# A hybrid encoder step on one core: attention in the source's order, value differences beside the gated mixer, keys first

## The chip, the cores and the metric

The kernel runs on one NeuronCore of one Trainium2 chip. The metric is the time of one execution on the device, in microseconds (us). Below, PE is TensorE, DVE is VectorE, ACT is ScalarE, POOL is GpSimd, and SP is the queue that issues most transfers.

## The reference

One layer of a streaming encoder works on 1024 prompt rows and 32 sample rows of width 1024:

```
xn     = RMSNorm(h);  u_a, u_b, v_b, q, k, v, gates = split(xn @ w_in)
y_a    = S5(u_a)                 # diagonal complex state space, scan over time, GELU, GLU
y_b    = u_b * (tril(W_s) @ LayerNorm(v_b) + b_s)          # gated mixer, chunks of 128
y_c    = stick_breaking(q, k, v)                           # 8 heads x 64, strictly causal
merged = sum_i sigmoid(gates_i) * (y_i @ w_branch_i);  h += merged @ w_out
h     += (silu(g) * u) @ w_down,  g, u = split(RMSNorm(h) @ w_gate_up);  y = RMSNorm(h)
```

Stick-breaking weights a value with sigmoid(z) times the product of (1 - sigmoid(z)) over the later keys. The outputs include keys, values and S5's final states.

## The kernel before, in words

Dense products are made three times in fp32r, with high and low parts of both operands (`mm3`, L143 to L146); weights are loaded, rounded on ACT (L117) and their rest is taken on POOL (L118) in a ring of four.

Phase 1 (L204 to L1060) projects the values (`v_dense`), then runs three things in the source's order: the S5 set-up on DVE (`s5_setup`), the gated mixer (`sgu`, nine blocks), the S5 main stage (`ua_dense`, `s5_main`), and then `attention`. Beside them runs filler: `tasks` holds four key/query tasks (`qk_dense`, one per pair of heads) and eleven gate tasks (`gate_ahead`). `fill(us)` (L1021) takes steps from the first task until their nominal cost, 3n/2400 us for n columns, has used up the credit; `finish` runs a task to its end. Before the change, the first two key/query tasks are finished before the mixer, the others are filler beside the mixer and S5. Tile's scheduler then orders each engine's instructions by source position and by its own forecast of readiness, so an instruction can come ahead of others that wait. SBUF pools that are closed give their place to later ones, and a tile waits for the tiles whose place it takes.

`qk_dense` splits keys and queries into high and low parts (`qe`, L325 to L330) and stores them by SP (L332). `s5_setup` builds S5's direct matrix D by sixteen transfers from `KK` (L632). `s5_main` loads U in eight transfers (L654), multiplies (L661), scans on DVE (L671 to L697), makes y (L708 to L710), stores and reloads it (L721, L726), and rounds it (`yh`, L729).

`attention` (L762) works in 32 units (pair of heads, pair of 128-row blocks tp, head). `stage_a` makes the scores of two row blocks on PE (L823 to L827), the sigmoid of minus the score on ACT (L829), and the reversed running product on DVE (L831, `om`). `stage_b` makes, for each pair of key blocks, a `turn` (four transposes, L853; their high part on ACT, L861; their low part on DVE, L862) and one turn later an `apply` (four products with the value differences, L870 and L871). It works with differences of neighbouring values: per head `load_values` loads two shifted copies (L780, L781) and `differences` makes them (L786 to L790). The next unit's `stage_a` steps are put between the turns of this one. `sample_attention` (L952) comes before the last unit; `while tasks: fill(1.0)` then runs what filler is left.

Phase 2 (L1065 on) loads the branch outputs y (L1095) and weighs them with the gates; three units of gate 7 come first there.

Of the kernel before, what the change touches and what calls it, by code (L numbers as in the profile page):

```python
# [9 lines left out]
F32 = mybir.dt.float32  # L10
F32R = mybir.dt.float32r
# [37 lines left out]
def trunk_kernel(ctx: ExitStack, tc: tile.TileContext,  # L49
# [32 lines left out]
    v_d = [dram.tile([TP + 1, 128], F32, name=f"v_d{i}") for i in range(4)]  # L82
    vs_d = dram.tile([32, 512], F32, name="vs_d")
# [120 lines left out]
    with ExitStack() as ph1:  # L204
# [3 lines left out]
        kk = ph1.enter_context(pool("kk", 1))  # L208
# [82 lines left out]
        def qk_dense(wk, hp):  # L291
# [22 lines left out]
            for which in (1, 0):  # L314
                unit = next_unit(768 + 512 * which + 128 * hp)
                dst = (q_d, k_d)[which][hp]
                for h, o, n, t0 in CHUNKS:
# [7 lines left out]
                    qe = wk.tile([128, 2, 512], F32R, name="qe", bufs=2)  # L325
# [30 lines left out]
        def sgu(wk, WT, BB, gs):  # L356
            pt = ps_tile("t")
            for i in range(4):
# [3 lines left out]
                            compare_op=OP.is_ge, fill=0.0)  # L362
            VN = wk.tile([128, 9, 256], F32, name="VN")
            us = tm_units(win, 512)
            for b, (t0, rows, h, off) in enumerate(BLOCKS):
# [20 lines left out]
                fill(1.5)  # L386
            for ft in range(2):
# [33 lines left out]
        def s5_setup(pl, keep, out):  # L421
# [185 lines left out]
            KK = pl.tile([32, 8, 128], F32, name="KK", tag="big")  # L607
# [154 lines left out]
        def attention(at, qk_tasks):  # L762
            cnt = [0]

            last = at.tile([128, 1], F32, name="last")
            v.tensor_scalar(last, ident[:, 127:128], -1.0, None, op0=OP.add)
# [6 lines left out]
            def load_values(hp, h2):  # L773

                va = at.tile([128, 12, 64], F32, name="va", bufs=1)
                vt = at.tile([128, 12, 2, 64], F32R, name="vt", bufs=3)
                vb = vt[:, :, 1, :].bitcast(F32)
                for tl, r0 in ((va, 0), (vb, 1)):
                    src = v_d[hp][r0:r0 + TP, 64 * h2:64 * h2 + 64].rearrange("(b s) c -> s b c", s=128)
                    sp.dma_start(tl[:, 0:8], src)  # L780
                    sp.dma_start(tl[:, 8:12], src[:, 1::2])  # L781
                return va, vt

            def differences(va, vt):
                vb = vt[:, :, 1, :].bitcast(F32)
                v.tensor_sub(va[:, 0:8], va[:, 0:8], vb[:, 0:8])  # L786

                v.scalar_tensor_tensor(va[:, 8:12], vb[:, 8:12], last, va[:, 8:12], op0=OP.mult, op1=OP.add)
                s.activation(vt[:, :, 0, :], va, AF.Copy)
                v.tensor_sub(vt[:, :, 1, :], va, vt[:, :, 0, :].bitcast(F32))  # L790
# [3 lines left out]
            diags = [[at.tile([128, 512], F32R, name=f"wd{i}{e}") for e in range(2)] for i in range(2)]  # L794
# [5 lines left out]
            raw_values = []  # L800
# [8 lines left out]
            def stage_a(hp, tp, h2):  # L809
                kst = heads[hp, h2][0]  # L810
                q2 = qs.pop((hp, tp, h2))
                ws = []
                for tt in range(2):
                    i = 2 * tp + tt
                    n = 128 * (i + 1)
                    cs = ((0, max(n, 256)),) if n <= 512 else (((0, 384), (384, 256)) if n == 640 else
                                                             ((0, 384), (384, 384)) if n == 768 else
                                                             ((0, 512), (512, n - 512)))
                    om = at.tile([128, 1024], F32, name="om", bufs=4)
                    for c0, w in cs:  # L820
                        z = ps_tile("z")
                        last = c0 + w >= n
                        pe.matmul(z[:, 0:w], q2[:, 0, 128 * tt:128 * tt + 128], kst[:, c0:c0 + w], start=True, stop=False)  # L823
                        pe.matmul(z[:, 0:w], q2[:, 1, 128 * tt:128 * tt + 128], kst[:, c0:c0 + w], start=False, stop=not last)
                        if last:
                            d0 = n - 128 - c0
                            pe.matmul(z[:, d0:d0 + 128], identb, maskb, start=False, stop=True)  # L827
                        e = min(w, n - c0)
                        s.activation(om[:, c0:c0 + e], z[:, 0:e], AF.Sigmoid, scale=-0.125)  # L829
                    rev = om[:, 0:n][:, ::-1]  # L830
                    v.tensor_tensor_scan(rev, rev, rev, 1.0, op0=OP.mult, op1=OP.bypass)  # L831
                    ws.append(om)
                    yield ws, 2 * n / 2400.0 + 0.06

            avs = {}

            def stage_b(hp, tp, h2, ws):
                vt = heads[hp, h2][1]
                if h2 == 0:
# [3 lines left out]
                hl = {}  # L843

                def turn(p):

                    pt = ps_tile("t")
                    diag = p == tp
                    for e in range(4):
                        if diag and e == 0:  # L850
                            continue
                        sb, tt = 2 * p + 1 - e // 2, e % 2
                        pe.transpose(pt[:, 128 * e:128 * e + 128], ws[tt][:, 128 * sb:128 * sb + 128], ident)  # L853
                    lo = 128 if diag else 0
                    if diag:
                        wh, wl = diags[cnt[0] % 2]
                        cnt[0] += 1
                    else:
                        wh = at.tile([128, 512], F32R, name="wth", bufs=2)
                        wl = at.tile([128, 512], F32R, name="wtl", bufs=2)  # L860
                    s.activation(wh[:, lo:512], pt[:, lo:512], AF.Copy)  # L861
                    v.tensor_sub(wl[:, lo:512], pt[:, lo:512], wh[:, lo:512].bitcast(F32))  # L862
                    hl[p] = wh, wl

                def apply(p):
                    wh, wl = hl.pop(p)
                    for i in range(2):
                        b = 8 + p if p == tp and i == 0 else 2 * p + 1 - i
                        lhs = vt[:, b].rearrange("p l d -> p (l d)")
                        pe.matmul(av, lhs, wh[:, 256 * i:256 * i + 256], start=(p == 0 and i == 0), stop=False)  # L870
                        pe.matmul(av, lhs, wl[:, 256 * i:256 * i + 256], start=False, stop=(p == tp and i == 1))  # L871

                for p in range(tp + 1):
                    turn(p)
                    yield 0.44
                    if p:
                        apply(p - 1)
                        yield 0.44
                apply(tp)
                if h2:  # L880
# [5 lines left out]
                    v.tensor_sub(yo[:, 1], ty, yo[:, 0].bitcast(F32))  # L886
                    o = 256 * (tp % 2)
                    for e in range(2):
                        sp.dma_start(y_d[4 + hp][tp // 2].rearrange("l p t -> p l t")[64 * e:64 * e + 64, :, o:o + 256],
                                     yo[:, :, 256 * e:256 * e + 256].bitcast(F32))  # L890
                yield 0.44

            units = [(hp, 3 - tp if hp == 3 else tp, h2) for hp in range(4) for tp in range(4) for h2 in range(2)]
            ratio = 0.7

            def run_a(u):
                for ws, c in stage_a(*u):
                    fill(ratio * c)
                return ws

            def ahead(i):

                if i < len(units):
                    hp, tp, h2 = units[i]
                    new = (hp, h2) not in heads
                    if new:
                        finish(qk_tasks[hp])
                        heads[hp, h2] = [load_head(hp, h2)]
                    load_q(hp, tp, h2)
                    if new:  # L910
                        while raw_values:
                            differences(*raw_values.pop())
                        pair = load_values(hp, h2)
                        heads[hp, h2].append(pair[1])
                        raw_values.append(pair)
                        return
                while raw_values:
                    differences(*raw_values.pop())
# [4 lines left out]
            ws = run_a(units[0])  # L923
            for i, u in enumerate(units):
                ahead(i + 2)
                nxt, done = None, True
                if i + 1 < len(units):
                    nxt = stage_a(*units[i + 1])
                    done = False
                for c in stage_b(*u, ws):  # L930
                    fill(ratio * c)
                    if not done:
                        try:
                            wn, c = next(nxt)
# [368 lines left out]
```

## Time and profile before

| | |
|---|---|
| median of 3 runs | 1789.54 us (1789.34 to 1792.63) |
| profiled execution | 1793.48 us, span 1791.7 us |
| PE, DVE, ACT, POOL busy | 95%, 39%, 29%, 30% of the span |
| mean granted PE clock | 0.974 of 2.4 GHz |
| PE waits before attention (75 to 450 us), listed | 28.7 us |
| PE waits from 450 to 705 us, listed | 26.2 us |

Times in rows are us from the span's start. "x8" counts instructions, and an arrow reads out<-in. A busy PE need not be at its peak: matmuls overlap, and their ends are modelled.

### The profile page before, as it was taken

The page shows a single profiled execution, that of the slowest core. Times are in us where ns is not written, and L with a number is a line of the kernel's source. Part 1 is how long each engine was busy: PE and PEld are TensorE (multiplying, and loading weights), DVE is VectorE, ACT ScalarE, POOL GpSimd, SP SyncE. Part 2 cuts the span into 40 slices and gives each one's busy share as a digit, 9 for nine tenths or more (in the row PEclk, how much of TensorE's full clock was granted, in tenths as well). Part 3 has the DMA queues.
Part 4 walks back from the last instruction along what each step waited for, and adds up shares of the span by engine and source line. Part 5 has one row for each costly group of instructions (what it writes and reads, how often), then busy time and mean ns, then how long its engine had stood idle before and what let it go on. Part 6 is the DMA issues. An engine that isn't in the chain of part 4 may idle for free.

```text
span 1791.7 us, 25639 instructions
## 1 busy us (share of the span) xinstructions
PE 1697.7 (95%) x10421; PEld 1504.1 (84%) x10421; DVE 698.9 (39%) x1396; ACT 520.7 (29%) x914; POOL 541.1 (30%) x333
## 2 busy tenths in 40 slices
PE   6988998999889899999999899999999999999997
PEld 6977897778677788899999798888889889888885
DVE  7962523312699840820275602131131230221215
ACT  4322332123466632222333321112112112111124
POOL 2210221334010323434452233333233323333344
PEclk9988999699999999999999999999999999999999
DMA  7453245255666526753362211111111111111112
GB/s 221 115 131 76 85 129 126 69 155 174 172 145 162 150 78 217 255 192 97 92 205 60 59 48 48 48 48 48 48 46 49 36 36 48 48 48 48 48 32 90
DMA packets 246575, 178.18 MB, mean 99 GB/s; under 512 B 60148, under 2 KB 223000, under 8 KB 246456
## 3 DMA queue, kind: packets, MB, share of 16 engines
q1 hardware_dynamic: 217896, 161.32, 31.1%
q10 hardware_dynamic: 28560, 15.21, 2.9%
q8 instruction: 82, 1.34, 0.3%
q14 instruction: 37, 0.30, 0.1%
HBM read 136.69 MB, written 39.21 MB: 98 GB/s over the span
## 4 chain that ended last, share of the span: by engine, by line
PE 75%; DVE 14%; issue 4%; DMA 3%; ACT 2%; POOL 1%; SPq 1%; POOLq 0%; ACTq 0%; DVEq 0%
PE p L146 18%; PE p L145 18%; PE p L144 18%; DVE om L831 4%; PE p_d L144 3%; PE p_d L146 3%; PE p_d L145 3%; PE p_av L144 2%; PE p_av L146 2%; PE p_av L145 2%; DVE rs_m L169 1%; DVE wtl L862 1%; PE p L1245 1%; DMA raw<-in_w_in_dram 1%; POOL wl L118 1%
## 5 line engine op out<-in xcount | busy, mean ns | idle before, releaser
L118 POOL TENSOR_TENSOR wl<-raw,wh 128x1024 fp32r<-128x1024 f32 x164 | 409.0, 2501 | 887.4 <-ACT wh L117 847.1
L145 PE MATMUL p<-x,wh 128*128 128x272 f32 (+1 forms) x1056 | 342.2, 324 | 0.0
L146 PE MATMUL p<-x,wl 128*128 128x272 f32 (+1 forms) x1056 | 341.4, 323 | 0.0
L144 PE MATMUL p<-x,wh 128*128 128x272 f32 (+1 forms) x1056 | 341.2, 323 | 0.0
L117 ACT ACTIVATE wh<-raw 128x1024 fp32r<-128x1024 f32 x164 | 172.6, 1060 | 463.8 <-PE p L146 178.9
L1201 DVE TENSOR_TENSOR sl<-p,sl 128x272 f32<-128x272 f32 (+1 forms) x66 | 34.7, 525 | 463.8 <-PE p L146 463.8
L144 PEld LDWEIGHTS p<-x,wh 128*128 128x128 f32 x1056 | 198.7, 188 | 16.0
L145 PEld LDWEIGHTS p<-x,wh 128*128 128x128 f32 x1056 | 198.7, 188 | 15.9
L146 PEld LDWEIGHTS p<-x,wl 128*128 128x128 f32 x1056 | 198.5, 188 | 15.2
L144 PE MATMUL p_d<-xnh,wh 128*128 128x272 f32 (+1 forms) x464 | 158.5, 342 | 10.9 <-ACT vb L377 7.2
L146 PE MATMUL p_d<-xnh,wl 128*128 128x272 f32 (+1 forms) x464 | 155.8, 336 | 4.7 <-POOL wl L118 4.7
L145 PE MATMUL p_d<-xnl,wh 128*128 128x272 f32 (+1 forms) x464 | 155.4, 335 | 0.0
L1204 POOL TENSOR_TENSOR act<-sl,act 128x512 fp32r<-128x512 f32 (+2 forms) x66 | 61.0, 925 | 278.7 <-ACT act L1202 278.7
L1255 DVE TENSOR_TENSOR h<-p,h 128x512 f32<-128x512 f32 x160 | 108.2, 687 | 79.2 <-PE p L146 79.2
L145 PE MATMUL p<-wl,act 128*128 128x512 f32 x352 | 137.2, 390 | 1.2 <-POOL wl L118 1.2
L146 PE MATMUL p<-wh,act 128*128 128x512 f32 x352 | 137.1, 389 | 0.0
L144 PE MATMUL p<-wh,act 128*128 128x512 f32 x352 | 136.9, 389 | 0.0
L144 PEld LDWEIGHTS p_d<-xnh,wh 128*128 128x128 f32 x464 | 90.1, 194 | 20.0 <-ACT vb L377 7.4
L146 PEld LDWEIGHTS p_d<-xnh,wl 128*128 128x128 f32 x464 | 89.6, 193 | 13.3 <-POOL wl L118 6.0
L145 PEld LDWEIGHTS p_d<-xnl,wh 128*128 128x128 f32 x464 | 90.2, 194 | 7.3
L831 DVE TENSOR_TENSOR_SCAN om<-om 128x128 f32<-128x128 f32 (+3 forms) x64 | 88.8, 1399 | 17.5 <-ACT om L829 17.4
L1202 ACT ACTIVATE act<-sl 128x272 fp32r<-128x272 f32 (+1 forms) x66 | 32.6, 494 | 189.7 <-DVE sl L1201 189.7
(414 smaller groups left out, 3360.3 us busy)
## 6 DMA issues: line engine op xcount, KB each, us to landing
raw<-in_w_in_dram SPq DMA_DIRECT2D x66, 512.0 KB, 3.9
raw<-in_w_gate_up_dram SPq DMA_DIRECT2D x44, 512.0 KB, 3.8
raw<-in_w_down_dram SPq DMA_DIRECT2D x22, 512.0 KB, 3.5
q<-q_d SPq DMA_DIRECT2D x64, 128.0 KB, 2.9
raw<-in_w_out_dram SPq DMA_DIRECT2D x16, 512.0 KB, 6.1
sig_d<-sga ACTq DMA_DIRECT2D x21, 256.0 KB, 2.7
sgg<-sig_d SPq DMA_DIRECT2D x21, 256.0 KB, 3.5
y<-y_d SPq DMA_DIRECT2D x16, 272.0 KB, 4.7
```

The source lines that it names most:

```text
L117: s.activation(wh, raw, AF.Copy)
L118: g.tensor_sub(wl, raw, wh.bitcast(F32))
L144: pe.matmul(ps, ah, bh, start=start, stop=False)
L145: pe.matmul(ps, ah, bl, start=False, stop=False)
L146: pe.matmul(ps, al, bh, start=False, stop=stop)
L169: v.scalar_tensor_tensor(t, y, mh, y, op0=OP.mult, op1=OP.mult)
L831: v.tensor_tensor_scan(rev, rev, rev, 1.0, op0=OP.mult, op1=OP.bypass)
L862: v.tensor_sub(wl[:, lo:512], pt[:, lo:512], wh[:, lo:512].bitcast(F32))
L1201: v.tensor_mul(sl[:, 0:n], pu, sl[:, 0:n])
L1202: s.activation(act[:, e, t0:t0 + n], sl[:, 0:n], AF.Copy)
L1204: g.tensor_sub(act[:, e, T + TS + t0:T + TS + t0 + p], sl[:, 0:p], act[:, e, t0:t0 + p].bitcast(F32))
L1255: v.tensor_add(hr[:, cs], ps, hr[:, cs])
```

## The change

Attention's instructions on PE and DVE are kept in the source's order (a manual schedule for those two engines). `stage_a` becomes `scores(u, tt)`; a unit's turns are followed by the next unit's two score blocks, and products come two turns after their transposes, across units, so there are three buffers for the high and low parts and three diagonal pairs. `fill` takes 2.0 nominal us per unit. The output's last subtraction and its stores come one turn later. Sample attention comes behind the last unit.

The value differences are made beside the gated mixer, one head per block, in a pool `vd` with one buffer of each kind, written to DRAM (`dv_d`) in one transfer per head and loaded in one in attention. All four key/query tasks are finished before the mixer, and the pool of their keys is closed there. The gates' prefetch is three units deep in the S5 main stage, where it was two, and the split keys have three buffers, where they had two.

```diff
+    dv_d = [dram.tile([128, 12, 2, 64], F32, name=f"dv_d{i}") for i in range(NH)]
...
-                    qe = wk.tile([128, 2, 512], F32R, name="qe", bufs=2)
+                    qe = wk.tile([128, 2, 512], F32R, name="qe", bufs=3)
...
+            def load_values(i):
+                va = vk.tile([128, 12, 64], F32, name="vda")
+                vt = vk.tile([128, 12, 2, 64], F32R, name="vdt")
+                for r0, tl in enumerate((va, vt[:, :, 0, :].bitcast(F32))):
+                    src = v_d[i // 2][r0:r0 + TP, 64 * (i % 2):64 * (i % 2) + 64].rearrange("(b s) c -> s b c", s=128)
+                    sp.dma_start(tl[:, 0:8], src)
+                    sp.dma_start(tl[:, 8:12], src[:, 1::2])
+                held.append((i, va, vt))
+            def differences():
...
+                v.tensor_sub(va[:, 0:8], va[:, 0:8], vb[:, 0:8])
+                v.scalar_tensor_tensor(va[:, 8:12], vb[:, 8:12], last, va[:, 8:12], op0=OP.mult, op1=OP.add)
+                s.activation(hi, va, AF.Copy)
+                v.tensor_sub(vt[:, :, 1, :], va, hi.bitcast(F32))
+                sp.dma_start(dv_d[i], vt.bitcast(F32))
...
                 fill(1.5)
+                if held:
+                    differences()
+                if b < 8:
+                    load_values(b)
...
-            KK = pl.tile([32, 8, 128], F32, name="KK", tag="big")
+            KK = pl.tile([32, 8, 128], F32, name="KK", tag="tg")
...
             def load_values(hp, h2):
...
+                sp.dma_start(vt.bitcast(F32), dv_d[2 * hp + h2])
+                return vt
...
             for i, u in enumerate(units):
                 ahead(i + 2)
+                nxt = units[i + 1] if i + 1 < len(units) else None
+                wn = []
+                part = beside / (u[1] + 2)
+                for p in range(u[1] + 1):
+                    held.append(turn(u, ws, p))
+                    if nxt and len(wn) < 2:
+                        wn.append(scores(nxt, len(wn)))
+                    if late:
+                        store()
+                    if len(held) > 2:
+                        apply(*held.pop(0))
+                    fill(part)
+                if nxt and len(wn) < 2:
+                    wn.append(scores(nxt, len(wn)))
+                fill(part)
+                qs.pop(u)
+                ws = wn
+            for h in held:
+                fill(2)
...
+                apply(*h)
...
+            sample_attention(at)
...
+                finish(qk_tasks[3])
+            with pool("sgu", 1) as sg, pool("vd", 1) as vk:
+                sgu(sg, vk, *sgc)
             with pool("s5m", 1) as s5m:
                 ua_dense(s5m)
-                unit_depth[0] = 2
+                unit_depth[0] = 3
                 s5_main(s5m, S)
         early[0] = False
+        with pool("at", 1) as at, tc.manual_schedule(engines={mybir.EngineType.PE, mybir.EngineType.DVE}):
+            attention(at)
```

## Rows read from the trace of the kernel before

**Rows 1.** Timelines of ACT and PE: start, duration, instruction, at the segments' ends

```profile
139.78 0.38 ACT L326 ACTIVATE qe<-p_d 128x272 fp32r<-128x272 f32 x1
...
249.16 0.27 ACT L648 ACTIVATE ua<-p_av 128x32 f32<-128x32 f32 x1
...
291.08 0.68 PE L661 MATMUL p_z<-U,BT 128*64 128x133 f32 x8
...
450.38 0.36 PE L823 MATMUL p_z<-kst,q 128*128 128x256 f32 x1 [1.80 <-DMA q<-q_d]
...
700.18 0.72 PE L144 MATMUL p<-xnh,wh 128*128 128x512 f32 x1 [2.00 <-ACT wh L117]
```

**Rows 2.** Waits of PE, 75 to 450 us: total, times, longest

```profile
PE p_d L144 <- ACT vb L377: 7.2, 1, 7.2
PE p_t L305 <- ACT kt L307: 7.0, 1, 7.0
```

**Rows 3.** Windows: length, busy PE, PEld, DVE, ACT, POOL, then PE clock, DMA share, GB/s

```profile
169.20:180.00 10.80, 10.79 (x69) 10.79 (x70) 9.45 (x57) 4.92 (x20) 0.00 (x0) 0.75 0.01 2
180.00:249.40 69.40, 68.15 (x481) 61.70 (x480) 29.66 (x78) 22.07 (x47) 14.76 (x7) 1.00 0.30 94
...
460.00:480.00 20.00, 18.73 (x109) 14.78 (x110) 14.50 (x19) 10.70 (x22) 0.00 (x0) 1.00 0.68 176
500.00:520.00 20.00, 16.58 (x102) 14.93 (x103) 16.63 (x22) 9.19 (x19) 5.04 (x2) 0.83 0.51 124
```

**Rows 4.** Waits of PE, 450 to 705 us

```profile
PE p_av L871 <- DVE wtl L862: 13.7, 17, 2.8
PE p_t L853 <- DVE om L831: 6.1, 14, 0.9
```

**Rows 5.** Timeline of ACT: ends of filler chunks (idle before in brackets), and yh

```profile
399.45 0.60 ACT L1014 ACTIVATE sga<-p_d 128x512 f32<-128x512 f32 x1 [4.98 <-PE p_d L146]
...
402.42 1.98 ACT L729 ACTIVATE yh<-U 128x2144 fp32r<-128x2144 f32 x1
...
686.14 0.40 ACT L1014 ACTIVATE sga<-p_d 128x272 f32<-128x272 f32 x1 [2.61 <-PE p_d L146]
```

**Rows 6.** Timeline of SP: first and last of U's loads, and y's reload

```profile
255.12 0.42 SPq L654 DMA_DIRECT2D U<-us_d  x1
...
282.20 2.81 SPq L654 DMA_DIRECT2D U<-us_d  x3
...
386.07 0.45 SPq L726 DMA_DIRECT2D U<-ys_d  x1
```

**Rows 7.** DMA issues: count, KB each, median us from issue to landing

```profile
kst<-k_d SPq DMA_DIRECT2D x8, 512.0 KB, 4.5
...
va<-v_d SPq DMA_DIRECT2D x8, 256.0 KB, 7.7
vt<-v_d SPq DMA_DIRECT2D x8, 256.0 KB, 5.3
...
U<-us_d SPq DMA_DIRECT2D x8, 134.0 KB, 4.9
```

**Rows 8.** Tile va in 450 to 672 us (busy DVE, ACT); a scan's group by line

```profile
450.00:672.00 222.00, 18.63 (x24) 6.73 (x8) 0.98 0.54 140
...
L831 DVE TENSOR_TENSOR_SCAN om<-om 128x1024 f32<-128x1024 f32 x8 | 19.6, 2445 | 0.0
```

**Rows 9.** Tile p_d (filler's PSUM) from the first score to 672 us: PE, PEld, DVE, ACT

```profile
450.40:672.00 221.60, 82.40 (x436) 64.65 (x437) 0.00 (x0) 7.74 (x18) 0.98 0.54 140
```

**Rows 10.** Groups of POOL and DVE by line, 640 to 672 us

```profile
L980 POOL TENSOR_SCALAR_AFFINE_SELECT sgs<-sgs 32x32 f32<-32x32 f32 x8 | 1.7, 208 | 1.8 <-ACT sgs L974 1.5
...
L983 DVE TENSOR_TENSOR_SCAN oms<-oms 128x160 f32<-128x160 f32 x2 | 1.0, 492 | 13.6 <-POOL oms L980 13.6
```

**Rows 11.** Timeline of SP at the end of attention

```profile
679.62 12.93 SPq L1095 DMA_DIRECT2D y<-y_d  x16
692.84 1.60 SPq L113 DMA_DIRECT2D raw<-in_w_in_dram  x2
```

More of the change, by code (lines that the diff above doesn't have):

```diff
@@ L807, in load_q, with scores @@
                 qs[hp, tp, h2] = q2
-            def stage_a(hp, tp, h2):
+            def scores(u, tt):
+                hp, tp, h2 = u
                 kst = heads[hp, h2][0]
[L811 to L833, printed above, removed]
@@ new lines, in scores @@
+                for c0, w in cs:
+                    z = ps_tile("z")
+                    last = c0 + w >= n
+                    pe.matmul(z[:, 0:w], q2[:, 0, 128 * tt:128 * tt + 128], kst[:, c0:c0 + w], start=True, stop=False)
+                    pe.matmul(z[:, 0:w], q2[:, 1, 128 * tt:128 * tt + 128], kst[:, c0:c0 + w], start=False, stop=not last)
+                    if last:
+                        d0 = n - 128 - c0
+                        pe.matmul(z[:, d0:d0 + 128], identb, maskb, start=False, stop=True)
+                    e = min(w, n - c0)
+                    s.activation(om[:, c0:c0 + e], z[:, 0:e], AF.Sigmoid, scale=-0.125)
@@ new lines, in scores, with store @@
+                rev = om[:, 0:n][:, ::-1]
+                v.tensor_tensor_scan(rev, rev, rev, 1.0, op0=OP.mult, op1=OP.bypass)
+                return om
+            avs = {}
+            late = []
+            def store():
+                (hp, tp, h2), yo, ty = late.pop()
+                v.tensor_sub(yo[:, 1], ty, yo[:, 0].bitcast(F32))
+                o = 256 * (tp % 2)
+                for e in range(2):
+                    sp.dma_start(y_d[4 + hp][tp // 2].rearrange("l p t -> p l t")[64 * e:64 * e + 64, :, o:o + 256],
+                                 yo[:, :, 256 * e:256 * e + 256].bitcast(F32))
@@ new lines, in turn @@
+            def turn(u, ws, p):
+                tp = u[1]
+                pt = ps_tile("t")
+                diag = p == tp
+                for e in range(4):
+                    if diag and e == 0:
+                        continue
+                    sb, tt = 2 * p + 1 - e // 2, e % 2
+                    pe.transpose(pt[:, 128 * e:128 * e + 128], ws[tt][:, 128 * sb:128 * sb + 128], ident)
+                lo = 128 if diag else 0
+                if diag:
+                    wh, wl = diags[cnt[0] % 3]
+                    cnt[0] += 1
+                else:
+                    wh = at.tile([128, 512], F32R, name="wth", bufs=3)
+                    wl = at.tile([128, 512], F32R, name="wtl", bufs=3)
+                s.activation(wh[:, lo:512], pt[:, lo:512], AF.Copy)
+                v.tensor_sub(wl[:, lo:512], pt[:, lo:512], wh[:, lo:512].bitcast(F32))
+                return u, p, wh, wl
@@ L840, in stage_b, with apply @@
+            def apply(u, p, wh, wl):
+                hp, tp, h2 = u
+                if (hp, tp) not in avs:
                     avs[hp, tp] = ps_tile("av")
@@ L842, in stage_b @@
                 av = av2[:, 256 * h2:256 * h2 + 256]
[L843 to L880, printed above, removed]
+                vt = heads[hp, h2][1]
+                for i in range(2):
+                    b = 8 + p if p == tp and i == 0 else 2 * p + 1 - i
+                    lhs = vt[:, b].rearrange("p l d -> p (l d)")
+                    pe.matmul(av, lhs, wh[:, 256 * i:256 * i + 256], start=(p == 0 and i == 0), stop=False)
+                    pe.matmul(av, lhs, wl[:, 256 * i:256 * i + 256], start=False, stop=(p == tp and i == 1))
+                if h2 and p == tp:
                     yo = at.tile([64, 2, 512], F32R, name="yo")
@@ L910, in ahead @@
                     if new:
[L911 to L918, printed above, removed]
+                        heads[hp, h2].append(load_values(hp, h2))
             for i in range(2):
@@ L1031, in finish @@
                 fill(1.0)
-        qk_tasks = [qk_dense(qk, hp) for hp in range(4)]
-        tasks.extend(qk_tasks)
-        tasks.extend(gate_ahead(qk, h, m) for h in range(2) for m in range(AHEAD[h]))
         with pool("s5k", 1) as s5k:
             sgc = sgu_consts(s5k)
-            with pool("s5t", 1) as s5t, pool("pv", 1) as pv:
+            with pool("s5t", 1) as s5t, pool("pv", 1) as pv, pool("kk", 1) as kk:
+                qk_tasks = [qk_dense(qk, kk, hp) for hp in range(4)]
+                tasks.extend(qk_tasks)
+                tasks.extend(gate_ahead(qk, h, m) for h in range(2) for m in range(AHEAD[h]))
                 S = {}
```

103 lines of the change are left out of this document (34 added, 69 removed).

## The prediction

> **What bounds the kernel now.** I read the busy shares first, then PE's waits by stage, then the boundaries of the stages in the timelines, then the queues. TensorE (PE) is busy nearly everywhere, so the time is its work plus what it loses: waits, and stretches at the lower clock. The change touches only the part up to phase 2. I cut that part into three segments at events that can be found again: the end of the second key/query task (139.8 us), the end of the S5 input projection (249.4), the first score matmul (450.4) and phase 2's first matmul (700.2) [rows 1]. Their lengths are 109.6, 201.0 and 249.8 us.
>
> The losses: 7.2 us at 162 to 169 on the gated mixer's first eviction, and 7.0 us before 105 us on a key eviction [rows 2]. After the first of them PE's granted clock averages 0.75 over 10.8 us in which PE is busy throughout [rows 3]: half of that time at 1.2 GHz, 2.7 us lost. In attention the listed waits are mainly 13.7 us on the low parts (wtl) and 6.1 us on the scans [rows 4].
>
> **The filler.** Key/query and gate tasks are drawn on by a nominal cost, so the source tells how much filler stands where. I counted it through the loops: four key/query tasks are 89.5 us, the gates 172.2, together 261.7. What it really costs: a 512-column gate chunk ends 4.98 + 0.60 = 5.58 us after the one before it, against 5.12 nominal; a 272-column one 2.61 + 0.40 = 3.01 against 2.72 [rows 5]. The factors are 1.09 and 1.11.
>
> **Segment A** (139.8 to 249.4). Before, 15.7 nominal us of the third key/query task run in it. After, tasks three and four (44.4) and the nine blocks' fills (13.5) do: +42.2 x 1.09 = +46.0. The 7.2 us wait and its 2.7 us of clock go: it ended on the copies into the S5 matrix D, which stood in SP's queue behind a key store that waited for PE; now 46 us of dense work lie between those copies and the gated mixer. That is -9.9. The third buffer for the split keys lets ScalarE run one chunk further past VectorE's late subtraction; between nothing and all of the 7.0 us I take the middle, -4. Sum +32: the input projection ends at 281.
>
> The values move into this segment: per head four loads, three VectorE operations, one on ScalarE, one store on SP. VectorE is 43% busy in 180 to 249 [rows 3] and hides its 2.3 us per head, provided the data is there when it asks: behind a late value subtraction stand the normalisations that free the eviction buffers, and behind a value load that waits for its buffer SP holds gate weights and U's loads. I cost this at nothing, at worst 1 us per head (8). The third diagonal pair, the new place of the small S5 kernel and the closed key pool issue nothing new, and cost nothing.
>
> **Segment B** (to 450.4). If PE is the bound: the filler executed in it is 121.2 nominal before, and 90.8 as placed after; -30.4 x 1.09 = -33.1, so 167.9 us, ending at 281 + 168 = 449. But the S5 chain must fit as well. Today U's eight loads are spread from 255 to 285 us [rows 6], between key and query stores that wait for dense work; without those they need about 5 us of issue. U's product can then start at 281 + 0.4 + 4.5 (the store's landing, as the 512 KB key load's) + 4.8 + 4.9 (a U load's landing) [rows 7] = 296. From that product to the first score it is 159.3 us now [rows 1]. Of these, 11 are ScalarE reaching yh only at 402.4 [rows 5], behind evictions of filler, though its load was issued at 386.07 [rows 6] and U's loads land in 4.9. So 148, and the chain ends at 444 if nothing holds its buffers.
>
> The value pool may hold them. It lies where the S5 main stage puts its fourth buffer, so V, W or Q wait for the eighth head. With one va and one vt buffer the heads go one after the other: 0.6 issue and 5.3 landing of vt [rows 7], 18.6 / 8 = 2.3 on VectorE and 0.84 on ScalarE [rows 8], 0.4 of hops, and a 768 KB store, nearest the key load's 4.5 and taken as 4.9. That is 14.3; bounds 12.4 (no issue, no hops, the store as 4.0) and 18.9 (vt's landing as va's 7.7, the store longer in proportion). From about 187 us on, 8 x 14.3 ends at 301, and 301 + 148 = 449. PE's own bound and the chain agree; I take **448** against 450.4. The third prefetched unit should remove weight waits in this segment; I leave that inside the 148.
>
> **Segment C** (first score to phase 2). Before, the last product ends at 672: 221.6 us, of it 436 filler matmuls [rows 9], 66 of 512 columns and 370 of 272, so 15.3 + 46.6 = 62 us, and 8 of sample attention. Attention's own time is 151.6, stalls included. In the change's favour: 18.6 us of value work leave VectorE [rows 8], and a product two turns late has no wtl to wait for (13.7). Against it: in source order a unit's first transposes come right behind the next unit's second score block, and need its sigmoid and its scan (0.6 + 2.4 at 1024 columns [rows 8], 0.3 of hops) with 2 to 2.5 us of products and filler between. Some 1 us at each of 31 unit changes is a loss of the old size. I take 151.6 unchanged; bounds -21 (nearly all listed waits gone) and +20. The filler left is 67.9 nominal, x 1.11 = 75.4: 227 us.
>
> Sample attention now comes last and without filler: the count runs dry during the last products, where 24.8 nominal us used to remain. Its chain is 1.4 + 2 x (1.35 scores + 0.6 sigmoids + 1.7 to 2.0 selects + 0.8 scan and product + 0.3 transposes + 0.55 copies + 1.84 products + 0.65 hops) = 17.6, of it the selects and the scan in [rows 10]. The y loads take 13 us of SP [rows 11]; phase 2's first three gate units (3 x 5.58 = 16.7) cover them if their weights are loaded ahead of y, which I expect because the weight ring is free early. C = 227 + 17.6 = 244.6, so phase 2 starts at 692.6, **7.6 us** earlier.
>
> The profiled execution took 1793.5 us, the median of three is 1789.5: 1785.9 on the profile's scale, **1782** on the median's.
>
> **A rule against it.** In 500 to 520 us, which holds a wait of 2.8 us, the granted clock is 0.83; in 460 to 480, where the waits are short, it is 1.00 [rows 3]. The Trainium skill ("TensorE: Matmul & The Clock Gate", Part 1) says that the throttled state is the default and that activity releases it. For the long wait the trace agrees; for short ones it shows no cost.
>
> **Rivals.** (1) *The values hold S5's buffers*, slower. At t us per head the first score is at 187 + 8t + 148, and the change loses from t = (700.2 - 244.6 - 335) / 8 = 15.1 on; at 16.5 it gives 1789.5 + 11 = 1801. For it: small pieces, 7.7 us of landing at worst. Against: the queues are emptier there than in attention. 0.22. (2) *Attention comes near its work*: filler hides the scans, -21 more, 1761. For it: VectorE is busy 16.6 of 20 us in 500 to 520 [rows 3] with value work in it, so without that it is not the bound. Against: the order is rigid. 0.17. (3) *The tail*: gate weights queue behind the y loads as today (692.84 after 679.62 [rows 11]), +12, 1794. Against: today those weights wait for a ring that filler still uses. 0.09. (4) *Clock*: waits at unit changes hold PE at 1.2 GHz; half of the 31 at 1.6 us is +25, 1807. 0.07. The forecast keeps 0.45.
>
> **Numbers.** About 0.2%, 3.6 us, is what a measurement of this kernel can tell from no change. The forecast spreads by some 8 us: 0.38 faster, 0.07 same. Rival 1: 0.18 slower, 0.04 same. Rival 2: 0.17 faster. Rival 3: 0.04 slower, 0.05 same. Rival 4: 0.06 slower, 0.01 same. Faster 0.55, same 0.17, slower 0.28. The range goes from rival 2 (with 3 us of its bound), 1758, to rival 1 at 16.5 with a little of rival 4, 1804.
>
> **What would show it.** Right: no wait of 7 us at the gated mixer's first block; U's loads within 10 us; the first score at 440 to 456; waits on wtl under 4 us and on the scans over 15; phase 2 near 693. Wrong: V or W waiting for a value store, the eighth of which ends after 310; a PE gap of over 15 us between the last product and phase 2; a clock below 0.95 in attention.

## The result, and the profile after

The changed kernel takes 1836.1 us (median of four runs, 1835.1 to 1837.1) against 1789.4: a ratio of 1.0257, 95% interval 1.024 to 1.0275. Its profiled execution took 1837.1 us, its span is 1835.3. The forecast of 1782, its range and its side are all wrong.

The ends of the segments, in ACT's and PE's timelines, answer to [rows 1]:

```profile
138.02 0.38 ACT L328 ACTIVATE qe<-p_d 128x272 fp32r<-128x272 f32 x1
...
312.82 0.29 ACT L678 ACTIVATE ua<-p_d 128x32 f32<-128x32 f32 x1
...
344.89 1.18 PE L691 MATMUL p_z<-U,BT 128*64 128x133 f32 x16
...
498.84 0.55 PE L833 MATMUL p_z<-kst,q 128*128 128x256 f32 x1 [14.19 <-DMA q<-q_d]
...
739.72 0.80 PE L147 MATMUL p<-xnh,wh 128*128 128x512 f32 x1
```

| segment | before | forecast | after | after - forecast |
|---|---|---|---|---|
| up to the second key/query task | 139.8 | 139.8 | 138.0 | -1.8 |
| A, to the end of the S5 input projection | 109.6 | 141.2 | 175.1 | +33.9 |
| B, to the first score | 201.0 | 167.0 | 185.7 | +18.7 |
| C, to phase 2 | 249.8 | 244.6 | 240.9 | -3.7 |
| phase 2 to the end | 1091.5 | 1091.5 | 1095.6 | +4.1 |

Against the forecast's span (1791.7 - 7.6 = 1784.1) the last column adds up to the missing 51.2 us. Two thirds lie in A, a third in B. What PE waited for in 190 to 313 us (total, times, longest) answers to [rows 2]:

```profile
PE p_av L147 <- ACT ua L676: 9.3, 1, 9.3
PE p_d L147 <- ACT wh L120: 4.1, 1, 4.1
PE p_z L434 <- DVE yt L438: 2.5, 1, 2.5
PE p_av L149 <- POOL wl L121: 1.7, 1, 1.7
PE p_d L148 <- POOL wl L121: 1.2, 1, 1.2
```

The longest names ScalarE's eviction of the input projection (`ua`). Three timelines show why it came late: ACT, VectorE, and the first and last of the eight value stores on SP.

```profile
286.66 0.83 ACT L385 ACTIVATE vdt<-vda 128x768 fp32r<-128x768 f32 x1
...
301.24 0.84 ACT L385 ACTIVATE vdt<-vda 128x768 fp32r<-128x768 f32 x1 [11.80 <-DVE vda L384]
301.98 1.08 ACT L676 ACTIVATE ua<-p_av 128x512 f32<-128x512 f32 x1
```

```profile
287.52 2.51 DVE L386 TENSOR_TENSOR vdt<-vda,vdt 128x768 fp32r<-128x768 f32 x1 [3.91 <-ACT vdt L385]
...
300.11 0.69 DVE L382 TENSOR_TENSOR vda<-vda,vdt 128x512 f32<-128x512 f32 x1 [7.77 <-DMA vdt<-v_d]
```

```profile
208.73 0.34 SPq L387 DMA_DIRECT2D dv_d<-vdt  x1
...
303.10 0.33 SPq L387 DMA_DIRECT2D dv_d<-vdt  x1
```

Read backwards: the last head's load lands at 300.1 and releases VectorE's subtraction; that releases ScalarE's copy at 301.24, for which ScalarE had stood 11.8 us; the eviction behind it in the same queue runs at 301.98, and PE goes on at 303.1. Each head takes (303.10 - 208.73) / 7 = 13.5 us. Over the whole stretch the windows (length, busy PE, PEld, DVE, ACT, POOL, then PE clock, DMA share, GB/s; as [rows 3]) are:

```profile
190.00:313.00 123.00, 101.49 (x650) 90.07 (x649) 58.25 (x159) 38.92 (x81) 25.12 (x12) 0.92 0.68 186
...
381.00:412.00 31.00, 30.76 (x97) 23.13 (x97) 0.40 (x4) 3.47 (x6) 2.34 (x1) 0.50 0.11 33
...
716.00:740.00 24.00, 11.23 (x55) 8.49 (x54) 8.05 (x13) 6.58 (x11) 13.72 (x20) 0.60 0.44 130
```

21.5 of 123 us idle and the clock at 0.92. The third row is sample attention, bare. The waits of PE in 450 to 745 us answer to [rows 4]:

```profile
PE p_z L833 <- DMA q<-q_d: 14.2, 1, 14.2
PE p_t L865 <- DVE om L841: 13.4, 9, 3.2
PE p_t L984 <- DVE sgs L981: 11.3, 2, 5.9
PE p_t L147 <- ACT sgl L776: 5.2, 7, 2.0
PE p_t L865 <- DVE wtl L874: 5.0, 4, 1.8
```

The 14.2 us stand before the first score; a wait of 10.3 us for VectorE's `Q` stands earlier, at 371 to 381 us, ahead of S5's y products. The load that the first score waits for is issued on SP only behind the S5 output's stores:

```profile
486.96 3.88 SPq L787 DMA_DIRECT2D y_d<-yoa  x4
490.88 0.80 SPq L797 DMA_DIRECT2D kst<-k_d  x1
491.73 1.86 SPq L817 DMA_DIRECT2D q<-q_d  x2
```

In the kernel before the same chain is no shorter (stores 434.9, first score 450.4), but PE worked on filler through it and waited 1.8 us. Attention as a whole (windows), then its filler alone, by its PSUM tile, as [rows 9]:

```profile
498.80:715.70 216.90, 198.22 (x1454) 181.54 (x1455) 158.45 (x174) 118.68 (x240) 26.08 (x9) 0.97 0.47 134
...
498.80:715.70 216.90, 93.12 (x588) 81.86 (x588) 0.00 (x0) 10.00 (x25) 0.97 0.47 134
```

### The profile page after: what moved, and what is told of

The parts are those of the page before. It is cut to its first block, busy times and chain, and to the rows that moved or that the text cites. A ratio compares the mean times of both kernels' runs of the same rounds, so it can differ in the third digit from the quotient of the medians.

```text
span 1835.3 us, 25667 instructions
## 1 busy us (share of the span) xinstructions
PE 1700.5 (93%) x10421; PEld 1511.9 (82%) x10421; DVE 716.0 (39%) x1396; ACT 519.6 (28%) x914; POOL 539.1 (29%) x335
## 4 chain that ended last, share of the span: by engine, by line
PE 60%; DVE 6%; ACT 2%; DMA 2%; issue 2%; POOL 1%; SPq 0%; POOLq 0%; ACTq 0%; DVEq 0%
PE p L148 17%; PE p L149 17%; PE p L147 17%; DVE om L841 2%; PE p_t L865 1%; PE p L1245 1%; PE p_d L147 1%; PE p_d L148 1%; PE p_d L149 1%; DVE rs_m L172 1%; PE p_av L887 1%; POOL wl L121 1%; DMA raw<-in_w_out_dram 1%; PE p_av L888 1%; PE p_z L833 1%
## 5 line engine op out<-in xcount | busy, mean ns | idle before, releaser
L147 PE MATMUL p_d<-xnh,wh 128*128 128x272 f32 (+1 forms) x432 | 145.3, 336 | 3.9 <-ACT wh L120 2.2
L149 PE MATMUL p_d<-xnh,wl 128*128 128x272 f32 (+1 forms) x432 | 143.3, 332 | 1.7 <-POOL wl L121 1.7
L148 PE MATMUL p_d<-xnl,wh 128*128 128x272 f32 (+1 forms) x432 | 143.6, 332 | 0.0
L841 DVE TENSOR_TENSOR_SCAN om<-om 128x128 f32<-128x128 f32 (+3 forms) x64 | 93.4, 1459 | 20.5 <-ACT om L839 20.1
L147 PEld LDWEIGHTS p_d<-xnh,wh 128*128 128x128 f32 x432 | 84.1, 195 | 11.3 <-ACT wh L120 2.6
L149 PEld LDWEIGHTS p_d<-xnh,wl 128*128 128x128 f32 x432 | 84.2, 195 | 8.7 <-POOL wl L121 2.1
L148 PEld LDWEIGHTS p_d<-xnl,wh 128*128 128x128 f32 x432 | 84.1, 195 | 6.3 <-issue 0.2
L147 PE MATMUL p_av<-xnh,wh 128*128 128x512 f32 (+1 forms) x216 | 77.9, 361 | 10.4 <-ACT ua L676 9.3
```

The source lines that it names most:

```text
L147: pe.matmul(ps, ah, bh, start=start, stop=False)
L148: pe.matmul(ps, ah, bl, start=False, stop=False)
L149: pe.matmul(ps, al, bh, start=False, stop=stop)
```

## The experiments

Medians of kernel before in these comparisons: 1790.8 to 1791.9 us. Intervals are 95%.

**Values back into attention.** The pool `vd` and its calls go, `va` and `differences` return to `ahead()`; the fixed order stays. For room there are two diagonal pairs, so in the last unit one pair is overwritten ahead of its product; the work is the same.

```diff
-            with pool("sgu", 1) as sg, pool("vd", 1) as vk:
-                sgu(sg, vk, *sgc)
+            with pool("sgu", 1) as sg:
+                sgu(sg, *sgc)
```

> The changed kernel with the value differences back inside attention (as in the kernel before; two diagonal pairs instead of three, for room). Theory V (the values, one head after the other, hold ScalarE and VectorE in front of the input projection's evictions): the input projection ends at 280 to 292 us instead of 312.8, attention grows by 5 to 10 us, the whole 1805 to 1820. Theory O (the fixed order loses the time: nothing can be put in front of the first score or beside sample attention): within 8 us of 1836. Theory K (keys first loses it): the input projection still ends after 300, the whole above 1825.

1841.9 us, 1.0295 (1.024 to 1.035). The input projection ends at 291.1, as theory V said, and the first score is at 476.0 instead of 498.8. But attention, from the first score to the last product, takes 245.8 us instead of 217. PE's waits there:

```profile
PE p_t L856 <- DVE om L832: 25.6, 12, 5.0
PE p_t L856 <- DVE wtl L865: 11.3, 10, 1.8
```

So the values' move costs 22 us up to the input projection (PE's idle time from the second key/query task on is 21.5 us against 5.6, and its granted clock 0.94 against 0.98) and, under a fixed order, saves 29 in attention: PE waits longer there for scans (25.6 against 13.4 us), with the value work back in VectorE's queue. Theory V priced that side at 5 to 10 us, and its 1805 to 1820 failed. For the whole, the intervals of this run and of the changed kernel overlap.

**Keys first alone**, on the kernel before.

```diff
-            with pool("s5t", 1) as s5t, pool("pv", 1) as pv:
+            with pool("s5t", 1) as s5t, pool("pv", 1) as pv, pool("kk", 1) as kk:
...
+                finish(qk_tasks[3])
```

> The kernel before with keys first alone (all four key/query tasks before the gated mixer, their pool closed there, third split buffer, the small S5 kernel's other place). Theory K: 1800 or more, the loss sits ahead of the first score. Theories V and O: the order of filler alone moves little, 1780 to 1795; the input projection ends at 280 to 292 and the first score at 440 to 456.

1795.0 us, 1.0026 (1.0006 to 1.0045). The projection ends at 291.0 (expected 280 to 292), but the first score comes only at 483.0 (expected 440 to 456). Keys first is no large loss and no gain. Its own windows at the end of attention, against 26.18 of 28 us busy at clock 1.00 before (672 to 700 us):

```profile
674.00:700.00 26.00, 18.69 (x87) 14.75 (x87) 15.69 (x23) 7.53 (x16) 13.60 (x20) 0.56 0.39 107
```

The filler was spent earlier and is missing here.

**No fixed order**, the rest as changed.

```diff
-        with pool("at", 1) as at, tc.manual_schedule(engines={mybir.EngineType.PE, mybir.EngineType.DVE}):
+        with pool("at", 1) as at:
```

> The changed kernel without the fixed order in attention: the same source, PE and VectorE ordered by the scheduler. Theory O: the 14.2 us wait before the first score and most of the 24 us of sample attention are covered by filler, 1805 to 1818. Theory V: the input projection still ends at 305 to 318, and the whole stays above 1820, since only the 14 us can come back.

1810.6 us, 1.0116 (1.0071 to 1.0162): the order costs 25.5 us. Three waits apart:

```profile
PE p_av L147 <- ACT ua L676: 9.4, 1, 9.4
...
PE p_z L722 <- DVE Q L729: 10.4, 1, 10.4
PE p_z L833 <- DMA q<-q_d: 2.2, 1, 2.2
```

The values' wait stays (projection at 315.5), that for Q too; that before the first score goes. Theory O's number came true, theory V's floor of 1820 did not, but its wait is visible beside it: both losses are there. By the windows the order costs PE 16.9 us of idle time from the y products to the first score (23.5 against 6.6), 4.0 in attention (18.6 against 14.6), and sample attention is 24.0 us long instead of 16.6.

**Values beside keys three and four**, three buffers.

```diff
+                with pool("vd", 1) as vk:
+                    values(vk)
+                    finish(qk_tasks[3])
```

> The changed kernel with the value differences beside the third and fourth key/query task (three buffers, loads two heads ahead) instead of beside the gated mixer. Theory V: the input projection ends at 280 to 292, its 9.3 us wait is gone, the whole 1800 to 1818. Rival to it (any place for the values in front of S5 costs as much, through SP's queue): the key/query tasks take over 60 us instead of 52, or the projection ends after 300, and the whole stays above 1825.

1849.3 us, 1.0332 (1.0285 to 1.0379): a miss. The first value load leaves SP at 196.1, behind the last query stores and the copies into D, so the values run after the keys, not beside them. The mixer's first eviction comes only at 243.5, when the last heads are done, and PE waits for it:

```profile
PE p_d L147 <- ACT vb L379: 29.5, 2, 28.4
```

**The value arithmetic left out**, loads and stores kept.

```diff
-                v.tensor_sub(va[:, 0:8], va[:, 0:8], vb[:, 0:8])
-                v.scalar_tensor_tensor(va[:, 8:12], vb[:, 8:12], last, va[:, 8:12], op0=OP.mult, op1=OP.add)
-                s.activation(hi, va, AF.Copy)
-                v.tensor_sub(vt[:, :, 1, :], va, hi.bitcast(F32))
```

> The changed kernel with the value differences' arithmetic left out of the gated mixer: the four loads and the store of each head stay (the raw and the shifted values are stored as they come), so attention multiplies with other values. Theory V1 (the differences stand in VectorE's and ScalarE's queues, wait there for their loads, and hold the evictions behind them): PE's idle time from the second key/query task to the end of the input projection falls from 21.5 to 5 to 9 us, the projection ends at 287 to 295 instead of 312.8, the whole 1808 to 1820. Theory V2 (SP's queue: loads and stores of values delay weights and stores): the projection still ends after 303, the whole above 1826.

1815.7 us, 1.014 (1.0092 to 1.0189), 20 us under the changed kernel. The wait for `ua` falls from 9.3 to 1.0, the weight wait stays:

```profile
PE p_d L147 <- ACT wh L120: 4.3, 1, 4.3
...
PE p_d L147 <- ACT ua L668: 1.0, 1, 1.0
```

PE's idle time up to the projection is 8.1 us, as V1 said; the projection ends at 301.3, later than V1's 295, because filler was run ahead of it (1012 matmuls up to there instead of 988). S5's first product, which stands behind both, comes at 327.5 us, against 344.9 in the changed kernel and 324.2 with the values in attention; the first score, at 479.8, is 19 us earlier. So 17 of some 21 us are the instructions waiting in the queues of VectorE and ScalarE, and 3 what is left with SP's transfers alone.

**Filler placed by hand under the fixed order.**

```diff
-            fill(12)
+            fill(27)
-            beside = 2.0
+            beside = 1.1
```

> The changed kernel, fixed order kept, with filler placed otherwise: 27 instead of 12 nominal us ahead of the first score, 1.1 instead of 2.0 per unit, which leaves some 16 for sample attention. Theory O1 (a fixed order costs because filler can no more be drawn to where PE runs idle, so placing it by hand gives most back): the wait before the first score falls from 14.2 to under 4 us, sample attention from 24 to under 17, the whole 1808 to 1822. Theory O2 (attention's own waits take what is given, since they had that filler as cover): the listed waits in attention grow by 15 us or more, the whole 1826 to 1840.

1845.9 us, 1.031 (1.0259 to 1.036): O1 falls. Two waits, and attention's window:

```profile
PE p_t L865 <- DVE om L841: 24.1, 22, 2.5
PE p_z L833 <- DMA q<-q_d: 11.2, 1, 11.2
...
506.40:710.40 204.00, 170.81 (x1231) 152.50 (x1232) 152.84 (x174) 111.15 (x227) 17.02 (x6) 0.97 0.45 128
```

The wait for q fell by 3 us only; the waits on scans grew by 10.7 us. By the windows PE's idle time fell from 23.5 to 15.5 us between the y products and the first score and from 12.8 to 6.2 in sample attention, and rose from 18.6 to 33.2 in attention: it took what was given, as theory O2 said, though the whole is above O2's range as well.

**Values in attention, no fixed order, less filler per unit.** As the first experiment, with

```diff
-        with pool("at", 1) as at, tc.manual_schedule(engines={mybir.EngineType.PE, mybir.EngineType.DVE}):
+        with pool("at", 1) as at:
-            beside = 2.0
+            beside = 1.2
+                    if i == 31 and len(held) > 1:
+                        apply(*held.pop(0))
```

> Keys first and the new source order of attention, values in attention as before, no fixed order, 1.2 nominal us of filler per unit (some 28 left for sample attention). If the fixed order and the values' place are the two losses, what is left is keys first: 1783 to 1798, near the 1795 of keys first alone. If products two turns late cost by themselves, 1800 or more.

1797.8 us, 1.0038 (1.0018 to 1.0059): near keys first alone (1795.0, the intervals overlap). Products two turns late cost nothing that shows.

**No fixed order, less filler per unit**: the same two edits on the changed kernel, values early.

> The changed kernel without the fixed order and with 1.2 instead of 2.0 nominal us of filler per unit. Theory T (in that form the filler runs out ahead of sample attention, whose 16.6 us then lie open): sample attention is covered, the whole 1800 to 1806 against 1810.6. Rival: the filler was worth the same beside the units, 1808 to 1814.

1814.7 us, 1.0137 (1.008 to 1.0194): the rival, just above its range. Sample attention is covered, but from the first score to phase 2 this run and the one with 2.0 us per unit take the same 202 us: the filler was worth as much beside the units. The 4 us more arise mostly in phase 2.

**The order on one engine.** `engines={mybir.EngineType.PE}`, then `engines={mybir.EngineType.DVE}`.

> The changed kernel with the fixed order on PE alone; VectorE ordered by the scheduler. Theory P (what a fixed order costs is that PE can draw no later filler into a wait): 1828 to 1842, the wait before the first score stays above 10 us. Theory D (VectorE's order is what costs, its scans standing behind subtractions that wait): 1808 to 1820, the waits on scans fall from 13 to under 8 us.

> The changed kernel with the fixed order on VectorE alone; PE ordered by the scheduler. Theory P: 1806 to 1818, the wait before the first score under 5 us. Theory D: 1826 to 1842.

PE alone: 1832.0 us, 1.0239 (1.0188 to 1.029). VectorE alone: 1823.0, 1.019 (1.0138 to 1.0242). Against 1810.6 without order, PE's order costs 21 us and VectorE's 12, both together 25.5. The wait before the first score, first with PE's order alone, then with VectorE's:

```profile
PE p_z L833 <- DMA q<-q_d: 14.0, 1, 14.0
```

```profile
PE p_z L833 <- DMA q<-q_d: 2.4, 1, 2.4
```

Theory P holds for PE; that VectorE's order alone would be free was wrong.

**Sample attention out of the fixed order.**

```diff
-            sample_attention(at)
...
+        with pool("at", 1) as at:
+            with tc.manual_schedule(engines={mybir.EngineType.PE, mybir.EngineType.DVE}):
+                attention(at)
+            sample_attention(at)
```

> The changed kernel with sample attention taken out of the fixed order, everything else fixed. Theory S (a third of the order's price is that nothing can be put beside sample attention): the stretch from the last product to phase 2 falls from 24 to 12 to 18 us, the whole 1823 to 1831. Rival (there is nothing left to put there, the filler is spent): 1833 to 1839.

1831.3 us, 1.0234 (1.0173 to 1.0295). The stretch falls to 16.6 us, the whole by 4.8, at the edge of what was expected and with intervals that overlap; in the trace phase 2 takes 3.9 us more.

**Five heads early, three in attention, no fixed order.**

```diff
-                if b < 8:
+                if b < 5:
                     load_values(b)
```

> The changed kernel without the fixed order, and with only the first five heads' value differences beside the gated mixer, the last three in attention as before (two diagonal pairs). Theory V1: at 13.5 us per head from 195 the fifth head is done by 263, ahead of the input projection's evictions, so the projection ends at 286 to 294, and the whole is 1784 to 1796. Rival (each value head costs, wherever it stands): the projection ends after 300 or attention takes over 200 us, 1800 or more.

1796.8 us, 1.0042 (1.002 to 1.0064). The projection ends at 295.3, the wait for `ua` is gone: the values hold the evictions only through the heads that are late. Both numbers lie just outside theory V1's (294 and 1796). And with 1797.8 for all values in attention, though at less filler per unit, the early heads gain nothing that shows.

**More filler in S5's gap**, on the version just shown; a second time; and on keys first alone.

```diff
             Z = W
-            fill(12)
+            fill(17)
...
-            fill(12)
+            fill(17)
             fin = pl.tile([128, 4, 8], F32, name="fin")
```

> The version with five heads early and no fixed order, with 17 instead of 12 nominal us of filler at each of the two places between V and the y products of S5. Theory G (keys first loses its gain in the 10.4 us wait for Q, since more of the filler is spent before it): the wait falls to under 2 us and the whole by 6 to 10 us, to 1786 to 1792. Rival (filler put there is missed later in the same amount): 1793 to 1800.

> Keys first alone (values in attention, no fixed order, the kernel before otherwise) with 17 instead of 12 nominal us of filler at the two places in S5. Theory F (the place of the filler gives the gain, whatever the values do): 1783 to 1790, under keys first alone by 5 us or more. Rival (five heads early give it): 1792 to 1799.

> The version with five heads early and the larger filler in S5, once more and beside the run above. If the earlier 1785.3 is real: 1782 to 1789 and below before with its interval; if it was the spread of runs: 1790 to 1798.

On five heads early: 1785.3 us, 0.9976 (0.9946 to 1.0006), and in the second run 1786.2, 0.9974 (0.9957 to 0.9991). On keys first alone: 1800.7, 1.0055 (1.0038 to 1.0072). This version beats both kernels, by some 0.25%, clear of no change in the second run alone, and not for the reason given: the wait for Q stays.

```profile
PE p_z L722 <- DVE Q L729: 12.4, 1, 12.4
```

Phase 2 starts at 696.5 and, in the second run, 695.4 us with the larger filler and at 695.3 without; the difference in the spans (4.4 and 8.7 us) arises after that. Most of it stands in phase 2's first 100 us, here without the larger filler and then in the second run with it:

```profile
695.30:795.30 100.00, 92.31 (x471) 78.55 (x471) 49.93 (x59) 23.38 (x27) 36.28 (x15) 0.94 0.75 247
...
695.40:795.40 100.00, 98.82 (x556) 86.02 (x556) 48.16 (x63) 23.39 (x28) 36.68 (x16) 0.97 0.74 246
```

PE is idle 7.7 us in the first and 1.2 in the second. Theory G and theory F fall; why filler in S5 shortens the waits of phase 2 stays open.

**Filler among the y products**, on that version and on the kernel before.

```diff
+                fill(2)
                 s.activation(Y.rearrange("p (a b) n -> p b a n", b=2)[:, h2, gs[0]:gs[-1] + 1, 0:133],
```

> The same with 2 nominal us of filler more behind each of the six groups of y products. Theory Y (these products alone do not keep PE's clock up, 0.50 over 29 us; dense work between them raises it): the clock over the y products is above 0.8, and the whole falls by another 5 to 12 us. Rival (the y products hold the clock down whatever stands between): the clock stays below 0.65, within 4 us of the run without.

> The kernel before with 2 nominal us of filler behind each of the six groups of y products, nothing else. Theory Y: the clock over the y products rises from 0.55 to above 0.8 and the whole falls by 5 to 12 us, to 1778 to 1786. Rival: within 4 us of before.

1791.2 us, 1.0000 (0.9978 to 1.0022), and 1797.5, 1.0042 (1.002 to 1.0063). Hardly any filler came to stand among the products: none in the second run, where they take 30.8 us against 28.9 before, and 17 matmuls in the first. There the windows over all y products, ahead of most of this filler and behind it are

```profile
369.00:402.00 33.00, 32.76 (x110) 24.88 (x110) 0.41 (x4) 3.96 (x7) 1.56 (x1) 0.58 0.01 4
...
380.00:392.00 12.00, 12.00 (x39) 9.11 (x39) 0.00 (x0) 1.01 (x2) 0.00 (x0) 0.50 0.00 0
...
398.00:402.00 4.00, 4.00 (x21) 3.16 (x21) 0.00 (x0) 1.94 (x3) 1.56 (x1) 1.00 0.07 27
```

So where dense filler did stand, the clock rose behind it, from 0.50 to 1.00; that is one place, and the whole is 5.9 us slower than without. Theory Y's gain is not shown. In the second run PE's wait for Q grew, first before, then with the filler:

```profile
PE p_z L692 <- DVE Q L699: 0.9, 1, 0.9
...
PE p_z L692 <- DVE Q L699: 10.1, 1, 10.1
```

That wait, then, comes without keys first too; what sets it stays open.

**Scores ahead of the turn**, fixed order kept.

```diff
-                    held.append(turn(u, ws, p))
                     if nxt and len(wn) < 2:
                         wn.append(scores(nxt, len(wn)))
+                    held.append(turn(u, ws, p))
```

> The changed kernel, fixed order kept, with the next unit's scores and scan issued ahead of a turn's transposes instead of behind them. Theory D (VectorE's order makes PE wait for scans, 13.4 us): the waits on scans fall under 6 us, the whole 1822 to 1831. Rival (the low parts are late instead): waits on the low parts rise over 10 us, 1832 to 1845.

1835.8 us, 1.0241 (1.0219 to 1.0262): no change.

```profile
PE p_t L865 <- DVE om L841: 10.3, 7, 2.7
PE p_t L865 <- DVE wtl L874: 10.3, 7, 2.8
```

What the scans gained (3.1 us), the low parts lost (5.3).

## Why the prediction was wrong

The four versions with keys first that differ in the two other parts, in us (at 1.2 nominal us of filler per unit the lower left one takes 1814.7):

| | no fixed order | fixed order |
|---|---|---|
| values in attention | 1797.8 (1.2 filler per unit) | 1841.9 |
| values beside the mixer | 1810.6 | 1836.1 |

**Segment A, the values "at nothing, at worst 1 us per head (8)".** This is the first failed step. They cost 22 us (projection at 313.1 against 291.1). The serial chain itself was forecast well: 14.3 us per head and an end at 301; it measured 13.5 and 303. The text even named VectorE's queue, but only for the mixer's normalisations, and let S5's fourth buffer be the one thing that the eighth head holds. What it holds is ScalarE: the input projection's evictions stand behind its copy, and PE behind them. Rival 1 had the right cause at the wrong place: its price began at 15.1 us per head, while the loss was there at 13.5.

**"That is -9.9."** The 7.2 us wait came back as 4.1 + 1.2 us on the mixer's weights. The copies into D were still issued late, at 191.6 to 194.2 us, behind the last query stores, and the weights behind them: they moved along with the keys. With the values back in attention it is the same: 3.9 and 1.5 us. The -4 for the third split buffer was booked in the wrong segment: the 7.0 us wait that it stands for lies before 105 us. There it became

```profile
PE p_t L307 <- ACT kt L309: 5.3, 1, 5.3
```

and the first segment is 1.8 us shorter.

**"PE's own bound and the chain agree; I take 448."** The count of filler nearly held: 414 matmuls of 512 columns ran in B, 17.3 chunks, 88.3 nominal us against the 90.8 counted. What failed is that PE's idle time (length less busy time, by the windows) was kept at before's 13.9 us; it was 34.8, with 14.2 for q and 10.3 for Q. The forecast weighed the fixed order inside attention only. Its price, 25.5 us, lies largely at attention's two ends: ahead of the first score, where later filler can no more be drawn forward, and in sample attention. The wait for Q is not the order's, since it stays without it.

The chain was mispriced as well, and at its start most. U's product was forecast 14.6 us behind the projection and came 31.8 behind: U's loads took 11.9 us of issue on SP instead of 4.8,

```profile
315.88 11.91 SPq L684 DMA_DIRECT2D U<-us_d  x8
```

and then PE, which was never idle there, still ran gate filler up to 344.9. From U's product to the first score it took 154.0 us instead of 148: of the 11 us that `yh` was to gain, 2.8 came (13.6 us from the issue of its load to its start, against 16.4 before). The forecast had let that load of 1072 KB land like one of 134 KB, which no run shows, and two evictions of filler still ran on ScalarE in between.

**Segment C.** Own time of attention "unchanged" at 151.6: it measured 216.9 - 75.4 = 141.5, inside the bounds. The 75.4 us of filler held, by the forecast's own cost of a matmul: 588 matmuls, 12 of 512 and 576 of 272 columns, are 2.8 + 72.6 us. Sample attention, 17.6 in the forecast, took 24.0: its transposes wait 11.3 us for VectorE. Without the order the same steps took 16.6 us with 5.7 of such waits, at a clock of 0.65 against 0.60, so the clock can be only a small part of it. The waits on scans (13.4) and the low parts (5.0) missed narrowly what was named (over 15, under 4). That C came out within 4 us is partly luck: attention gained 10 us, and sample attention lost 6.

**Rivals.** Attention coming near its work gave half of its 21 us. A clock held down in attention did not happen (0.97). The tail was bare, but through the order and the spent filler, not through gate weights behind y. The chance of 0.28 for slower was too low: the evictions on ScalarE behind the values, the weights on SP behind the copies into D, and the load of q on SP behind S5's stores each stood in a queue behind something late, and none of the three had a price in the sum.

Open remain phase 2's 4.1 us more, what sets the wait for Q, and why VectorE's order alone costs 12 us.

## What to carry to other kernels

Work moved off the critical engine goes into somebody's in-order queue: list what stands behind each moved instruction at the time its load lands, not the engine's busy share. A hand-written order for PE also takes away the filler that the scheduler draws into waits; price its edges, where the order begins and ends, before its middle. And when two parts of a change hide each other (here the values' move costs 17 us without the fixed order, at equal filler, and nothing clear of noise under it), undo both, one at a time and together.

## What was not expected of the hardware

The y products of S5 run at a granted clock of 0.50, the 1.2 GHz level, for 31 us in which PE is busy 30.8 (windows above). In the changed kernel the clock had fallen during the 10.3 us wait ahead of them (0.76 on average from 371 to 381 us). The kernel before has no such wait (the last two ahead of them are 1.0 us each): its y products begin at 1.00 and drop to 0.50 while PE is busy throughout:

```profile
326.00:328.00 2.00, 2.00 (x13) 1.52 (x12) 0.28 (x1) 1.06 (x1) 0.00 (x0) 1.00 0.07 18
328.00:354.00 26.00, 26.00 (x83) 19.47 (x83) 0.00 (x0) 4.31 (x7) 6.24 (x3) 0.50 0.14 41
```

In the forecast a low clock followed a wait; here it falls and stays low while PE is not idle, and it comes back only with dense products, behind the y products in both kernels and among them in the run with filler there. The Trainium skill ("TensorE: Matmul & The Clock Gate", Part 1) says that activity releases the throttled state; the rows do not agree, if being busy is taken for activity, and the measurement decides.

A VectorE subtraction of 128x768, both inputs in SBUF, takes 0.96 us (median of eight) and took 2.51 from 287.52 on, while POOL split a weight tile from 286.83 to 289.21:

```profile
286.83 2.38 POOL L121 TENSOR_TENSOR wl<-raw,wh 128x1024 fp32r<-128x1024 f32 x1 [15.81 <-ACT wh L120]
```

The Trainium skill ("SBUF — State Buffer", "SBUF: two separate sides") says that the two engines share a port pair as an exclusive lock, held for the whole instruction. The trace agrees: 289.21 and 0.96 make 290.17, and the subtraction ended at 290.03.
